# A two-block network on one core: where the first stage makes its low weight parts, and in which order its last projection reads its input

## The chip, the cores and the metric

The kernel runs on one core of a Trainium2 chip. Its time is the device time of one execution in microseconds (us); the number used is the median of the runs shown. The engines are named as the profile names them: PE multiplies matrices (PEld is its weight load), DVE is the vector engine, ACT the scalar engine, POOL is GpSimd, SP the queue that issues most loads. L75 is line 75 of the kernel.

## The reference, cut to what matters

A sequence of 256 positions with 1024 channels passes through two blocks. The change lies in the first half of the first block:

```python
h = rms_norm(x, norm1_g)
q, k, v, a, g = split(h @ w_in, 5)            # five parts of 512 columns each
attn = neighbourhood_attention(q, k, v, rpb)
conv = conformer_conv(a, g, ...)              # a*sigmoid(g), 31 taps per channel, LayerNorm, silu
mixed = concatenate([rms_norm(attn), rms_norm(conv)])
x = x + mixed @ w_out
h = rms_norm(x, norm2_g)
x = x + expert_choice_ffn(h, ...)             # 16 experts, 24 MB of weights each
```

After it come a second attention with a gating branch, and 256 gathers of rows from a table of 16,384 experts.

## The kernel before, in words

**Products in two parts.** The first stage multiplies in a reduced format that keeps only the high part of an fp32 number. To keep precision each operand is split in a high and a low part, and each product is three matmuls: high by high, high by low, low by high (`TERMS`). A weight block of 128 x 1024 (four of them make one 1024 x 512 weight, `kp` 0 to 3) is split by `split_w`: ACT copies it to `wh` (L68), and another engine subtracts, `wl = w - wh` (L75). With `pool_every=n` every n-th subtraction goes to POOL, the rest to DVE. `wh` and `wl` have three buffers each, so a split can run three blocks ahead of PE.

**The order of the first stage.** The weights come in the order g, a, q, k, v, then `w_out` in two halves of 512 columns, with the 12 loads of `w_ada` (the modulation of the second block, tile `pa`, L270) spread between them. `proj_T` (matmuls at L93) makes g, a, q and k transposed, `proj_N` (L111) makes v and the last projection. In q, k and v all low parts are POOL's (`pool_every=1`); in g and a they are DVE's.

**What runs beside it.** After a and g, DVE computes the convolution of three of the four channel groups, one tap at a time: `acc` gets a first tap (L363) and 30 more (L366) for each group. The fourth group goes over PE with diagonal matrices made by ACT (`cdg`, L375, L376). The scores of the four head pairs (L430) go to DVE (L434, L436), the exponentials to ACT (L441), then transposes and products on PE (L452, L461). Convolution and attention are normed (`conv_norm`, `attn_norm`) and written by `mix_in` into `mixT`: chunks 0 to 3 hold the attention, 4 to 7 the convolution. `mix_in` makes the product on DVE (L418), the high part on ACT (L81), the low part on DVE (L82).

**The last projection.** `wo[0]` and `wo[1]` are the two halves of `w_out`. A block `kp` uses chunks 2kp and 2kp+1 of `mixT`, so blocks 0 and 1 belong to the attention, 2 and 3 to the convolution. Then `turn_rows` transposes the new `X` (L576), `pl` are the router's logits (L592), and the experts begin (L658, L693).

**What sets the order.** The text is written in program order, but a scheduler that works on the dependencies places each engine's instructions; each engine then runs its own list strictly in order. SP issues loads strictly in order too. A weight load waits until its slot is free: there are five slots of 2 MB (`wload`), and four more for the experts (`W2`) that open when the first stage's memory is given back.

The lines that the change touches in the calls before:

```python
for _ in proj_T(P1, wload(A["w_in"][0]), hl, q_evac, pool_every=1):
run(proj_N(P1, wo[0], mixT, res_evac(0), pool_every=2, order=(2, 3, 0, 1)))
```

Of the kernel before, what the change touches and what calls it, by code (L numbers as in the profile page):

```python
# [9 lines left out]
AF = mybir.ActivationFunctionType  # L10
# [26 lines left out]
def body(tc, A, out, x1_in=None, dump=None, parts="1234"):  # L37
# [3 lines left out]
    act = nc.scalar.activation  # L41
# [10 lines left out]
    def ps(shape=(128, 512), name="ps"):  # L52
        return PS.tile(list(shape), F32, name=name, tag="ps")

    def pq(shape=(128, 512), name="pq"):
        return PS.tile(list(shape), F32, name=name, tag="pp")
# [7 lines left out]
    def split_w(pl, raw, wl=None, pool_every=0, bufs=3):  # L64

        wh = pl.tile([128, 1024], F32R, name="wh", tag="wh", bufs=bufs)
        ref, both, he, le = gate.pop(0) if gate else (None, False, None, None)
        i = act(wh, raw, AF.Copy) if he is None else he.tensor_copy(out=wh, in_=raw)  # L68
        if both:
            after(i, ref)  # L70
        if wl is None:
            wl = pl.tile([128, 1024], F32R, name="wl", tag="wl", bufs=bufs)
        turn[0] += 1
        eng = le or (nc.gpsimd if pool_every and turn[0] % pool_every == 0 else nc.vector)
        i = eng.tensor_tensor(out=wl, in0=raw, in1=wh.bitcast(F32), op=OP.subtract)  # L75
        if ref is not None:
            after(i, ref)
        return wh, wl
# [5 lines left out]
    def proj_T(pl, wt, hl, evac, wl=None, pool_every=0):  # L84

        pp = [pq((128, 2, 256), name="pp") for _ in range(2)]
        for kp in range(4):
            wp = split_w(pl, wt[:, kp * 1024:(kp + 1) * 1024], None if wl is None else wl[:, kp * 1024:(kp + 1) * 1024], pool_every)
            for c in range(4):
                for k2 in range(2):  # L90
                    kd = kp * 2 + k2
                    for n, (a, b) in enumerate(TERMS):
                        mm(pp[c // 2][:, c % 2], lhsT=wp[a][:, k2 * 512 + c * 128:k2 * 512 + (c + 1) * 128],  # L93
                           rhs=hl[:, b, kd], start=kd == 0 and n == 0 and c % 2 == 0, stop=kd == 7 and n == 2,
                           skip_group_check=True)
            if kp < 3:
                yield
        for c2 in range(2):
            evac(c2, pp[c2])
        yield  # L100

    def proj_N(pl, wt, hl, evac, wl=None, pool_every=0, order=(0, 1, 2, 3)):

        pp = [pq(name="pp") for _ in range(2)]
        for i, kp in enumerate(order):
            wp = split_w(pl, wt[:, kp * 1024:(kp + 1) * 1024], None if wl is None else wl[:, kp * 1024:(kp + 1) * 1024], pool_every)
            for k2, t in ((0, 0), (0, 1), (1, 0), (1, 1)) if i < 3 else ((0, 0), (1, 0), (0, 1), (1, 1)):
                kd = kp * 2 + k2
                for n, (a, b) in enumerate(TERMS):
                    x = hl[b] if isinstance(hl, list) else hl[:, b]  # L110
                    mm(pp[t], lhsT=x[:, kd, t * 128:(t + 1) * 128], rhs=wp[a][:, k2 * 512:(k2 + 1) * 512],  # L111
                       start=i + k2 + n == 0, stop=i == 3 and k2 == 1 and n == 2)
            if i < 3:
                yield
        for t in range(2):
            evac(t, pp[t])
        yield

    def run(g):
        for _ in g:  # L120
            pass

    def after(ins, ref):

        tc.add_manual_dep(ins.ins, ref.ins.name, mybir.DependencyInfo(mybir.DependencyClass.Sync, mybir.DependencyReason.DATA),
                          reason="loads in the order of their use")
# [103 lines left out]
    def wload(src, n=4096, cut=1):  # L230
        if extra and extra.pop(0):
            t = W2.tile([128, 4096], F32, name="w", tag="w%d" % (3 - ring[2] % 4))
            ring[2] += 1
        else:
            i = ring[0] % ring[1]
            t = W.tile([128, 4096], F32, name="w", tag=("w", "w", "w", "wa", "wb")[i], bufs=3 if i < 3 else 1)
            ring[0] += 1
        dst = t[:, :n]
        if len(src.shape) == 3:
            dst = dst.rearrange("p (a b) -> p a b", a=src.shape[1])  # L240
        k = src.shape[1] // cut
        for i in range(cut):
            nc.sync.dma_start(out=dst[:, i * k:(i + 1) * k], in_=src[:, i * k:(i + 1) * k])
        return t
# [80 lines left out]
    if "1" in parts:  # L325
        p1 = ExitStack()
        P1 = p1.enter_context(pool(name="P1", bufs=1))
# [5 lines left out]
        hl = HP.tile([128, 2, 8, 256], F32R, name="h0", tag="h")  # L333
# [8 lines left out]
        def sl(c2):  # L342
            return slice(c2 * 2, c2 * 2 + 2)
# [4 lines left out]
        kT = P1.tile([128, 4, 256], F32, name="kT")  # L348
        vv = P1.tile([128, 2, 512], F32, name="vv")
# [38 lines left out]
                r = slice(hh * 64, hh * 64 + 64)  # L388
                act(qz[r, sl(c2), hh], p[r], AF.Copy)

        for _ in proj_T(P1, wload(A["w_in"][0]), hl, q_evac, pool_every=1):
            pass
        next(ad)
        run(proj_T(P1, wload(A["w_in"][1]), hl, lambda c2, p: act(kT[:, sl(c2)], p, AF.Copy), pool_every=1))

        next(ad)

# [67 lines left out]
        vev = []  # L465
        wv_ = wload(A["w_in"][2])
# [1 line left out]
        for i in range(4):  # L468
            nc.sync.dma_start(out=bias[:, i * 2:i * 2 + 2], in_=A["bias"][:, i * 2:i * 2 + 2])
        hps = [head_pair(hc) for hc in range(4)]  # L470
        for i, _ in enumerate(proj_N(P1, wv_, hl, lambda t, p: vev.append(act(vv[:, t], p, AF.Copy)), pool_every=1)):
            if i in (0, 2):
                next(hps[0])
            for _ in range(6):
                next(cv, None)
        mixT = HP.tile([128, 2, 8, 256], F32R, name="mixT", tag="h")
# [39 lines left out]
        wo = []  # L516
# [42 lines left out]
        def res_evac(b):  # L559
            def f(t, p):  # L560
                h = slice(b * 512, (b + 1) * 512)
                tt_(out=X[:, t, h], in0=p, in1=X[:, t, h], op=OP.add)
                after(act(hj[:, b, t * 512:(t + 1) * 512], X[:, t, h], AF.Square, accum_out=xss[:, t, b:b + 1]), early)
            return f
# [6 lines left out]
        def turn_rows(kp):  # L571
            p = ps((128, 2, 256))
            for k2 in range(2):
                for t in range(2):
                    kd = kp * 2 + k2
                    nc.tensor.transpose(p[:, k2, t * 128:(t + 1) * 128], X[:, t, kd * 128:(kd + 1) * 128], ident)  # L576
            act(h2[:, kp * 2], p[:, 0], AF.Copy)
            nc.vector.tensor_copy(out=h2[:, kp * 2 + 1], in_=p[:, 1])

        run(proj_N(P1, wo[0], mixT, res_evac(0), pool_every=2, order=(2, 3, 0, 1)))  # L580
        for i, _ in enumerate(proj_N(P1, wo[1], mixT, res_evac(1), pool_every=2)):
            if i in (1, 2):
                turn_rows(i - 1)
        turn_rows(2)
        turn_rows(3)
        pl = [pq((128, NE), name="pl") for t in range(2)]
# [246 lines left out]
    hl = HP.tile([128, 2, 8, 256], F32R, name="h1", tag="h")  # L833
# [11 lines left out]
    for t in range(2):  # L845
        i = nc.vector.tensor_scalar(out=xn[:, t], in0=X[:, t], scalar1=r2[:, t:t + 1], scalar2=None, op0=OP.mult)
# [126 lines left out]
    for kp in range(4):  # L973
        p = ps((128, 2, 256))
# [54 lines left out]
    for g2 in range(4):  # L1029
        p = ps((128, 2, 2, 128))  # L1030
        for g in range(2):
            for n in range(2):
                i = mm(p[:, g, n], lhsT=zv[:, n, (g2 * 2 + g) * 128:(g2 * 2 + g + 1) * 128], rhs=sws[:, g2 * 2 + g], start=True, stop=True)
# [17 lines left out]
    wo = [wload(A["w_out_2"][b]) for b in range(2)]  # L1051
    hl = HP.tile([128, 2, 8, 256], F32R, name="h2", tag="h")
# [459 lines left out]
```

## Time and profile before

| what | value |
|---|---|
| time, median of 3 runs (lowest to highest) | 2171.81 us (2170.49 to 2178.94) |
| the profiled execution's own time | 2175.27 us |
| its span, first to last instruction | 2173.3 us |
| busy PE, DVE, ACT, POOL | 1652.7, 918.4, 493.6, 509.8 us |
| mean DMA traffic | 361 GB/s |

The profiled execution is 3.46 us above the median. Part 2 of the page cuts the span in 40 slices of 54 us, each digit being busy tenths:

```profile
PE   7698767767666665555657999996888888887777
DVE  5934210000000000000006866766967766776754
POOL 3602100000000000000003311224555545554552
DMA  8578999999999999999996433436999999999996
GB/s 356 201 299 288 421 427 410 423 426 418 417 427 427 427 426 428 427 426 429 427 426 254 163 117 110 182 126 259 408 420 421 421 420 421 421 421 421 421 421 265
```

The first four slices are the first stage (up to some 204 us). From slice 5 to 22 the experts' weights come in at about 427 GB/s, then the second block follows, and from slice 28 on the gathers load DMA again. In the second slice PE, DVE and POOL are busy for 6 tenths and more while DMA moves only 201 GB/s.

### The profile page before, as it was taken

What the parts mean: (1) busy time and instruction counts of PE and PEld (TensorE: products, weight loads), DVE (VectorE), ACT (ScalarE), POOL (GpSimd) and SP (SyncE); (2) the same over time, 40 slices, a digit from 0 to 9 for tenths busy, and PEclk for the clock granted to TensorE, in tenths of its full rate; (3) what the DMA queues carried; (4) which work ended last, traced back from release to release, by engine and by line L of the source; (5) the groups of instructions that cost most, each with busy time, mean ns of one, the idle gap of its engine ahead of it and who ended that gap; (6) DMA issues with size and microseconds to landing.
All of it is one profiled execution on the core that took longest, in us unless ns stands there. A gap on an engine that the chain in (4) does not pass through costs nothing. (4 is left out here: it accounts for less than half of the span.)

```text
span 2173.3 us, 21500 instructions
## 1 busy us (share of the span) xinstructions
PE 1652.7 (76%) x8132; PEld 853.4 (39%) x8132; DVE 918.4 (42%) x1939; ACT 493.6 (23%) x985; POOL 509.8 (23%) x353
## 2 busy tenths in 40 slices
PE   7698767767666665555657999996888888887777
PEld 6555213222211111111115878985444433443332
DVE  5934210000000000000006866766967766776754
ACT  4373110000000000000004456642332222222111
POOL 3602100000000000000003311224555545554552
PEclk9898977889987788887888999997999999999998
DMA  8578999999999999999996433436999999999996
GB/s 356 201 299 288 421 427 410 423 426 418 417 427 427 427 426 428 427 426 429 427 426 254 163 117 110 182 126 259 408 420 421 421 420 421 421 421 421 421 421 265
DMA packets 81974, 784.90 MB, mean 361 GB/s; under 512 B 12752, under 2 KB 13136, under 8 KB 18640
## 3 DMA queue, kind: packets, MB, share of 16 engines
q1 hardware_dynamic: 39920, 508.25, 56.8%
q0 software_dynamic: 36864, 268.45, 29.8%
q10 hardware_dynamic: 5088, 6.84, 1.0%
q8 instruction: 64, 1.05, 0.2%
q14 instruction: 38, 0.31, 0.0%
HBM read 780.35 MB, written 3.16 MB: 361 GB/s over the span
## 5 line engine op out<-in xcount | busy, mean ns | idle before, releaser
L1329 PE MATMUL acc<-uv,dgu 128*128 128x512 f32 x1024 | 493.9, 639 | 119.1 <-ACT dgu L1327 119.0
L1303 POOL DMA_INDIRECT uv<-in_peer_uv_dram,ei x256 | 331.6, 1295 | 304.2 <-DMA uv<-in_peer_uv_dram,ei 149.9
L1311 DVE CUSTOM_DVE_ANT_0 uv<-uv,xn 128x1024 f32<-128x1024 f32 x256 | 313.3, 1225 | 150.6 <-DMA uv<-in_peer_uv_dram,ei 142.8
L1329 PEld LDWEIGHTS acc<-uv,dgu 128*128 128x128 f32 x1024 | 203.6, 204 | 380.2 <-issue 234.7
L710 PE MATMUL pd<-w,hidT 128*32 128x512 f32 x1024 | 175.9, 805 | 97.0 <-DMA w<-in_w_down_dram 89.5
L693 PE MATMUL pu<-w,xsT 128*32 128x512 f32 x1024 | 157.8, 745 | 101.3 <-DMA w<-in_w_up_dram 101.2
L693 PE MATMUL pg<-w,xsT 128*32 128x512 f32 x1024 | 154.1, 729 | 97.0 <-DMA w<-in_w_gate_dram 97.0
L699 DVE TENSOR_TENSOR hid<-pu,hid 128x512 f32<-128x512 f32 x16 | 11.1, 691 | 503.8 <-PE pu L693 470.0
L859 POOL MEMSET q2z<- 64x2048 f32 x1 | 1.8, 1798 | 865.4 <-PE pd L710 865.4
L93 PE MATMUL pp<-h,wh 128*128 128x256 f32 x896 | 172.3, 294 | 2.0 <-DVE h L82 1.1
L75 POOL TENSOR_TENSOR wl<-w,wh 128x1024 fp32r<-128x1024 f32 x34 | 106.5, 3133 | 242.7 <-ACT wh L68 242.3
L93 PEld LDWEIGHTS pp<-h,wh 128*128 128x128 f32 x896 | 145.2, 198 | 7.0 <-issue 1.9
L93 PE MATMUL pp<-h,wl 128*128 128x256 f32 x448 | 130.2, 291 | 22.5 <-POOL wl L75 19.8
L714 DVE COPY part<-pd 128x512 f32<-128x512 f32 x16 | 11.1, 692 | 283.1 <-PE pd L710 283.1
L68 ACT ACTIVATE wh<-w 128x1024 fp32r<-128x1024 f32 x99 | 104.1, 1058 | 94.0 <-PE pp L93 65.0
L710 PEld LDWEIGHTS pd<-w,hidT 128*32 128x32 f32 x1024 | 39.2, 130 | 217.3 <-DMA w<-in_w_down_dram 141.6
L693 PEld LDWEIGHTS pu<-w,xsT 128*32 128x32 f32 x1024 | 32.0, 124 | 223.1 <-DMA w<-in_w_up_dram 162.4
L1320 ACT ACTIVATE a<-dots 128x4 f32<-128x4 f32 (+1 forms) x66 | 13.6, 205 | 445.9 <-DVE dots L1311 445.9
L693 PEld LDWEIGHTS pg<-w,xsT 128*32 128x32 f32 x1024 | 30.5, 121 | 206.7 <-DMA w<-in_w_gate_dram 144.1
L698 ACT ACTIVATE hid<-pg 128x512 f32<-128x512 f32 x16 | 9.6, 597 | 446.5 <-PE pg L693 446.5
L75 DVE TENSOR_TENSOR wl<-w,wh 128x1024 fp32r<-128x1024 f32 x66 | 83.8, 1278 | 39.1 <-ACT wh L68 38.9
L93 PEld LDWEIGHTS pp<-h,wl 128*128 128x128 f32 x448 | 88.8, 198 | 23.5 <-POOL wl L75 20.4
(353 smaller groups left out, 2119.7 us busy)
## 6 DMA issues: line engine op xcount, KB each, us to landing
w<-in_w_up_dram SPq DMA_DIRECT2D x64, 2048.0 KB, 21.0
w<-in_w_gate_dram SPq DMA_DIRECT2D x64, 2048.0 KB, 21.1
w<-in_w_down_dram SPq DMA_DIRECT2D x63, 2048.0 KB, 21.6
w<-in_w_in_dram SPq DMA_DIRECT2D x22, 2048.0 KB, 8.6
w<-in_w_ada_dram SPq DMA_DIRECT2D x12, 2048.0 KB, 8.5
w<-in_w_out_dram SPq DMA_DIRECT2D x4, 2048.0 KB, 8.0
rw<-in_peer_w_query_dram SPq DMA_DIRECT2D x12, 512.0 KB, 8.4
w<-in_w_branch_attn_dram SPq DMA_DIRECT2D x2, 2048.0 KB, 7.6
```

Source lines behind the costliest of these rows:

```text
L68: i = act(wh, raw, AF.Copy) if he is None else he.tensor_copy(out=wh, in_=raw)
L75: i = eng.tensor_tensor(out=wl, in0=raw, in1=wh.bitcast(F32), op=OP.subtract)
L93: mm(pp[c // 2][:, c % 2], lhsT=wp[a][:, k2 * 512 + c * 128:k2 * 512 + (c + 1) * 128], rhs=hl[:, b, kd], start=kd == 0 and n == 0 and c % ...
L693: mm(p[j * 32:(j + 1) * 32, :], lhsT=xsT[:, kd, e * 32:(e + 1) * 32], rhs=w[:, k2 * 2048 + j * 512:k2 * 2048 + (j + 1) * 512], start=kd == ...
L698: first = act(hid, pg, AF.Silu)
L699: tt_(out=hid, in0=pu, in1=hid, op=OP.mult)
L710: mm(pd[h][j * 32:(j + 1) * 32, :], lhsT=hidT[:, q, j * 32:(j + 1) * 32], rhs=w[:, j * 1024 + h * 512:j * 1024 + (h + 1) * 512], start=q = ...
L714: nc.vector.tensor_copy(out=part[:, 512:1024], in_=pd[1])
L1303: nc.gpsimd.indirect_dma_start(out=r, out_offset=None, in_=UV, in_offset=bass.IndirectOffsetOnAxis(ap=eis[u][:, k:k + 1], axis=0))
L1311: nc.vector.tensor_tensor_reduce(out=x, in0=x, in1=hx[:, u % 2], scale=1.0, scalar=0.0, op0=OP.mult, op1=OP.add, accum_out=dots[:, j:j + 1])
L1320: act(a[:, 0:n], dots[:, 0:n], AF.Gelu)
L1329: mm(acc[t][b], lhsT=dg, rhs=r[:, D + b * 512:D + (b + 1) * 512], start=h == 0 and k == 0, stop=h == 7 and k == 15)
```

## The change

The three calls for q, k and v lose `pool_every=1`, so that their twelve low parts are made on DVE. The last projection no longer runs half by half with the convolution first in `wo[0]`; its two generators are stepped by hand: attention blocks of `wo[0]`, attention blocks of `wo[1]`, convolution blocks of `wo[0]`, convolution blocks of `wo[1]`. The transposes `turn_rows` 0 and 1 stand behind the last two steps.

```diff
-        for _ in proj_T(P1, wload(A["w_in"][0]), hl, q_evac, pool_every=1):
+        for _ in proj_T(P1, wload(A["w_in"][0]), hl, q_evac):
             pass
         next(ad)
-        run(proj_T(P1, wload(A["w_in"][1]), hl, lambda c2, p: act(kT[:, sl(c2)], p, AF.Copy), pool_every=1))
+        run(proj_T(P1, wload(A["w_in"][1]), hl, lambda c2, p: act(kT[:, sl(c2)], p, AF.Copy)))
...
-        for i, _ in enumerate(proj_N(P1, wv_, hl, lambda t, p: vev.append(act(vv[:, t], p, AF.Copy)), pool_every=1)):
+        for i, _ in enumerate(proj_N(P1, wv_, hl, lambda t, p: vev.append(act(vv[:, t], p, AF.Copy)))):
...
-        run(proj_N(P1, wo[0], mixT, res_evac(0), pool_every=2, order=(2, 3, 0, 1)))
-        for i, _ in enumerate(proj_N(P1, wo[1], mixT, res_evac(1), pool_every=2)):
-            if i in (1, 2):
-                turn_rows(i - 1)
+
+        g0 = proj_N(P1, wo[0], mixT, res_evac(0), pool_every=2)
+        g1 = proj_N(P1, wo[1], mixT, res_evac(1), pool_every=2)
+        for g in (g0, g0, g1, g1, g0, g0):
+            next(g)
+        for i in range(2):
+            next(g1)
+            turn_rows(i)
         turn_rows(2)
         turn_rows(3)
```

**DVE, from the end of the a projection to the taps.** `wl` are the low parts, `u` the gated input of the convolution, `acc` its sum. Before:

```order
L75 TENSOR_TENSOR wl<-w,wh 128x1024 x5
L353 TENSOR_TENSOR u<-pp,sg 128x2x256 x2
L363 TENSOR_SCALAR acc<-u,vec 128x256 x2
L366 SCALAR_TENSOR_TENSOR acc<-u,vec,acc 128x256 x60
L363 TENSOR_SCALAR acc<-u,vec 128x256
L366 SCALAR_TENSOR_TENSOR acc<-u,vec,acc 128x256 x15
```

The same place on DVE now:

```order
L75 TENSOR_TENSOR wl<-w,wh 128x1024 x7
L353 TENSOR_TENSOR u<-pp,sg 128x2x256 x2
L363 TENSOR_SCALAR acc<-u,vec 128x256
L75 TENSOR_TENSOR wl<-w,wh 128x1024
L366 SCALAR_TENSOR_TENSOR acc<-u,vec,acc 128x256
L363 TENSOR_SCALAR acc<-u,vec 128x256
L366 SCALAR_TENSOR_TENSOR acc<-u,vec,acc 128x256 x9
L75 TENSOR_TENSOR wl<-w,wh 128x1024
L366 SCALAR_TENSOR_TENSOR acc<-u,vec,acc 128x256 x3
L75 TENSOR_TENSOR wl<-w,wh 128x1024
L366 SCALAR_TENSOR_TENSOR acc<-u,vec,acc 128x256 x5
```

The two low parts of q's first blocks stand ahead of `u`, and each of the other ten stands between 3 to 10 taps; in this way it goes on to the last block of v, whose low part stands behind the first head pair's score `s` (L434).

**DVE, at the fourth head pair.** `s` are its scores, `st` its sums, `modT` a part of the second block's modulation, `rva` the variance of the convolution. Before:

```order
L75 TENSOR_TENSOR wl<-w,wh 128x1024 x2
L485 TENSOR_TENSOR acc<-acc,ps 128x256 x4
L434 SCALAR_TENSOR_TENSOR s<-ps,bias 128x512 x2
L436 TENSOR_REDUCE st<-s 128x2 x2
L281 TENSOR_TENSOR modT<-ps,vec 128x16 x2
L164 TENSOR_SCALAR rva<-ps 128x2
```

Now, behind the same pair's scores:

```order
L442 RECIPROCAL st<-st 128x2
L75 TENSOR_TENSOR wl<-w,wh 128x1024
L281 TENSOR_TENSOR modT<-ps,vec 128x16 x2
L164 TENSOR_SCALAR rva<-ps 128x2
L817 TENSOR_TENSOR gm_4311<-modT,vec 128x8
```

Before, this low part (the third of `w_out`) stood ahead of the fourth head pair's scores; it is now `wo[1]`'s first block, and ACT's high part for it stands between the pair's second and third exponential too.

**PE, at the start of the last projection.** `pp` are its sums, `dg` with `ones` spreads a row's scale over the partitions (convolution first, then attention), `sqs` with `ones` are the attention's sums of squares. Before:

```order
L413 MATMUL ps<-dg,ones 128x128 x2
L403 MATMUL ps<-ones,sqs 128x1 x8
L111 MATMUL pp<-wh,mixT 128x512 x3
L111 MATMUL pp<-wl,mixT 128x512
L111 MATMUL pp<-wh,mixT 128x512
L111 MATMUL pp<-wl,mixT 128x512
L111 MATMUL pp<-wh,mixT 128x512 x2
L111 MATMUL pp<-wl,mixT 128x512
L111 MATMUL pp<-wh,mixT 128x512
L413 MATMUL ps<-dg,ones 128x128
```

And now:

```order
L403 MATMUL ps<-ones,sqs 128x1 x8
L413 MATMUL ps<-dg,ones 128x128 x2
L111 MATMUL pp<-wh,mixT 128x512 x5
L111 MATMUL pp<-wl,mixT 128x512
L111 MATMUL pp<-wh,mixT 128x512
```

The attention's two `dg` products stood behind ten matmuls of the convolution's half; now they stand ahead of the first matmul of the projection. On POOL the row of 13 low parts shrinks to 1. SP's list of loads is the same in both.

## Rows read from the trace of the kernel before

**Rows 1.** PE in order of time, 52 to 77 us: start, length, engine, line, count.

```profile
52.80 0.40 PE L93 MATMUL pp<-h,wh 128*128 128x256 f32 x2
...
53.16 0.40 PE L93 MATMUL pp<-h,wh 128*128 128x256 f32 x2
72.25 0.58 PE L93 MATMUL pp<-h,wl 128*128 128x256 f32 x1 [18.69 <-POOL wl L75]
...
76.84 1.92 PE L270 MATMUL pa<-w,cT 128*32 128x512 f32 x16
```

**Rows 2.** POOL in order of time, up to 48 us.

```profile
43.70 2.38 POOL L75 TENSOR_TENSOR wl<-w,wh 128x1024 fp32r<-128x1024 f32 x1 [0.48 <-ACT wh L68]
```

**Rows 3.** POOL's instructions by line, 48 to 49 us: count | busy, mean ns | idle before.

```profile
L75 POOL TENSOR_TENSOR wl<-w,wh 128x1024 fp32r<-128x1024 f32 x1 | 23.5, 23522 | 2.6 <-ACT wh L68 2.6
```

**Rows 4.** Busy time by stretch: PE, PEld, DVE, ACT, POOL; PE's clock, DMA share, GB/s.

```profile
60.00:65.00 5.00, 0.00 (x0) 0.00 (x0) 5.00 (x14) 0.00 (x0) 5.00 (x1) 0.50 0.00 0
72.00:76.00 4.00, 3.75 (x17) 3.75 (x18) 3.93 (x3) 1.18 (x2) 4.00 (x3) 0.50 0.70 225
155.00:158.00 3.00, 3.00 (x20) 0.77 (x16) 0.00 (x0) 1.02 (x1) 0.00 (x0) 0.50 1.01 431
210.00:215.00 5.00, 5.00 (x37) 2.42 (x37) 0.75 (x1) 0.69 (x1) 0.00 (x0) 1.00 0.11 46
...
200.00:1220.00 1020.00, 681.96 (x3918) 233.66 (x3918) 137.03 (x204) 80.63 (x131) 38.10 (x28) 0.83 0.96 405
```

**Rows 5.** DVE in order of time, 13 to 107 us.

```profile
13.38 1.23 DVE L75 TENSOR_TENSOR wl<-w,wh 128x1024 fp32r<-128x1024 f32 x1
14.52 0.48 DVE L204 TENSOR_SCALAR hf<-ps,vec 128x256 f32<-128x256 f32 x1
...
42.68 0.69 DVE L353 TENSOR_TENSOR u<-pp,sg 128x512 f32<-128x512 f32 x1 [0.74 <-PE pp L93]
...
46.16 23.84 DVE L366 SCALAR_TENSOR_TENSOR acc<-u,vec,acc 128x256 f32<-128x256 f32 x60
...
96.16 0.69 DVE L434 SCALAR_TENSOR_TENSOR s<-ps,bias 128x512 f32<-128x512 f32 x1 [1.71 <-PE ps L430]
...
102.46 4.13 DVE L366 SCALAR_TENSOR_TENSOR acc<-u,vec,acc 128x256 f32<-128x256 f32 x8
106.51 1.28 DVE L434 SCALAR_TENSOR_TENSOR s<-ps,bias 128x512 f32<-128x512 f32 x2
```

**Rows 6.** DVE's taps by line: first 46 to 60 us, then 72.5 to 94.4 us.

```profile
L366 DVE SCALAR_TENSOR_TENSOR acc<-u,vec,acc 128x256 f32<-128x256 f32 x35 | 13.9, 482 | 0.0
...
L366 DVE SCALAR_TENSOR_TENSOR acc<-u,vec,acc 128x256 f32<-128x256 f32 x15 | 21.6, 1438 | 0.5
```

**Rows 7.** ACT in order of time, 50 to 142 us.

```profile
50.41 1.06 ACT L68 ACTIVATE wh<-w 128x1024 fp32r<-128x1024 f32 x1 [1.81 <-PE pp L93]
...
141.38 0.57 ACT L276 ACTIVATE m<-pa 128x512 f32<-128x512 f32 x1
```

**Rows 8.** PE in order of time, 163 to 191 us.

```profile
163.13 0.94 PE L111 MATMUL pp<-wh,mixT 128*128 128x512 f32 x3
...
166.28 0.40 PE L413 MATMUL ps<-dg,ones 128*128 128x128 f32 x2
...
187.36 0.39 PE L111 MATMUL pp<-wl,mixT 128*128 128x512 f32 x1
...
189.51 0.85 PE L576 MATMUL ps<-cst,X 128*128 128x128 f32 x6
```

**Rows 9.** DVE in order of time, 166 to 171 us.

```profile
166.72 1.26 DVE L418 SCALAR_TENSOR_TENSOR mf<-oT,vec,ps 128x256 f32<-128x256 f32 x3 [0.19 <-PE ps L413]
...
170.90 0.47 DVE L418 SCALAR_TENSOR_TENSOR mf<-oT,vec,ps 128x256 f32<-128x256 f32 x1
```

**Rows 10.** SP's load issues in order of time, 170 to 183 us.

```profile
170.05 0.33 SPq L243 DMA_DIRECT2D w<-in_w_gate_dram  x1
182.05 0.33 SPq L243 DMA_DIRECT2D w<-in_w_up_dram  x1
```

## The prediction

> **What bounds the kernel now.** I began with the digits of the page. From slice 5 on the expert weights fill DMA, so the first stage counts by when it lets the experts start. The stretches confirm it: over 200 to 1220 us DMA is at 0.96 of its share, while between 210 and 215 us it falls to 0.11 with PE busy throughout, since all slots are loaded and PE has only just begun to use them [rows 4]. From there on DMA waits for PE's start, and what comes earlier there ends earlier.
>
> Then I looked in the first stage for the engine that idles though it has work: PE in order of time. Its three-matmul groups of the q projection follow each other every 0.36 us (52.80 to 53.16), then it stands still for 18.69 us and waits for a low part from POOL [rows 1]. POOL's own rows say why: the subtraction takes 2.38 us when it runs alone [rows 2], and one that began under DVE's taps took 23.5 us [rows 3]. DVE was inside a run of 60 taps [rows 5] and never idle. During the wait DMA moved nothing (60 to 65 us), and PE's granted clock was 0.50, its 1.2 GHz level, and stayed there to 76 us [rows 4].
>
> **The change part by part.**
>
> *The wait goes.* Minus 18.69 us [rows 1]. The clock drop behind it goes as well. From 72.25 to 76.84 us PE ran the 21 matmuls left of q, 4.59 us [rows 1]; at 0.36 us for three they are 2.52 us, so another 2.1 us. Together 20.8 us, if the low parts come in time from DVE.
>
> *Do they come in time?* A low part on DVE takes 1.23 us and the next instruction starts 1.14 us after it began [rows 5]. Taps follow each other every 23.84/60 = 0.397 us when two channel groups alternate, and every 4.13/8 = 0.516 us when one group's chain is left [rows 5]. DVE is free at 43.4 us, when the second `u` is done (42.68 + 0.69) [rows 5]. From there by the new order: first tap and q's third low part to 44.9; eleven taps and q's fourth part, 44.9 + 4.4 + 1.1 = 50.5 us. PE needs it at 53.3, where it stopped before. k's first: three taps later, but its high part is on ACT until 51.5 (50.41 + 1.06) [rows 7]; done at 52.8, needed at 57.9 (q ends at 53.3 + 2.5, then 16 matmuls of `pa`, 1.92 us [rows 1]). A block of q or k is 24 matmuls, 2.88 us on PE, and between two low parts DVE has 3 to 10 taps, 1.2 to 4 us. Continued like this, k's fourth is there at 63.8 and needed at 66.5; v's first at 66.9 and needed at 71.4; v's last, behind the first head pair's score, at 77.4 and needed at 81.5. The smallest slack is some 2.5 us. So I count no stall of PE here; DVE reaches the first score at 75.5 us, against 96.16 minus 20.8 = 75.4 [rows 5].
>
> *What is late next.* The taps that stand between the first two head pairs: 16 of them, 38 in all to the third. The second pair's scores come on DVE at about 86.3 us; moved by 20.8 us they stood at 106.51 - 20.8 = 85.7 [rows 5]. ACT's exponentials wait for them: plus 0.6 us. Bounds: 0, if PE's diagonal products hide it, and 6.9 us, worked out under the second rival.
>
> *The third split of `w_out`.* It moves from a place where ACT and DVE were waiting into the fourth head pair's exponentials. ACT makes a high part in 1.06 us [rows 7], and `m`, for which PE waits, now comes behind one: PE's transposes of `m` are followed in its order by the convolution's sums, so that chain slips by 1.06 us and some of what DVE adds (1.23 us ahead of `modT` and `rva`). I take 1.7 us; bounds 0 (the slack between ACT's pieces) and 1.06 + 1.23 = 2.3 us.
>
> *The last projection.* PE began it at 163.13 us with the convolution's half and did ten matmuls before the first of the attention's two spreads; the second began at 166.28 [rows 8]. The attention's product came on DVE from 166.72 on, the last piece at 170.90 [rows 9]. Now PE has nothing to do until the attention's high part is there. The spreads run at once, at about 165.6 to 166.1; the products begin at some 166.4 (0.4 us each, three in 1.26) [rows 9], ACT's copy is 0.4 us: the first matmul is at 167.2 us. The sums: 96 matmuls stood with 8 transposes and 4 spreads from 163.13 to 187.59 (187.36 and one step) [rows 8], 24.5 us; less 12 small ones, 96 are 22.3 us. Now 4 transposes come in between (0.6 us), from 167.2: 190.1 us. On top comes the clock: PE does only the one-column sums of squares and four spreads for some 5 us ahead of 167.2. After the convolution's like sums the clock stood at 0.50, the 1.2 GHz level, from 155 to 158 us [rows 4]. Some 3.6 us of half pace cost 1.8 us. Bounds for the clock: 0, if it holds, and 2.1 us, as after the long wait. So 191.9 against 187.59: plus 4.3 us. Behind the last matmul four more transposes stand in front of the router, by 0.85 us for six [rows 8] plus 0.6 us.
>
> *Loads.* SP's order is unchanged, but `wo[0]`'s slot now comes free with its last low part, some 9 us later than the 170.05 us at which a gate load took it, and `wo[1]`'s about 2.5 us later than 182.05 [rows 10]. Behind it queue the loads for expert 0. PE itself is 5 us later here, so I take nothing; the DMA gap of 210 to 215 us [rows 4] covers it. Without that cover it would cost up to one load, 4.9 us at 427 GB/s.
>
> Sum: -20.8 + 0.6 + 1.7 + 4.3 + 0.6 = -13.6 us, so 2175.27 - 13.6 = 2161.7 for the profiled execution. That one lies 3.46 us above the median; from 2171.81 the forecast is 2158.2, rounded to **2158 us**. With the bounds (clock, split, pair) its own range is 2152 to 2163.
>
> **The rivals.**
>
> *The whole 20 us.* The last projection and the split cost nothing, because the attention is ready earlier than its old place in the queues shows: 2171.8 - 20.2 = 2151.6 us. For it: PE works through the old start without a long wait, and DVE's queue is emptier without POOL's subtractions. Against it: the attention's spread depends on `rva`, which stands behind the convolution's products on DVE in both orders.
>
> *DVE paces the stage.* Each tap takes 482 ns itself [rows 6], and the pace of 0.397 us holds only as long as the next one starts before the last has ended. The Trainium skill, "VectorE: DVE Perf Modes", section "The DRAIN you can't avoid", says that the next instruction cannot issue until the pipe has emptied; by that rule the pace is the duration. This trace differs, 60 taps in 23.84 us, and I go by it. At 0.482 us instead: 54 instructions up to the first score, each 0.085 us more, are 4.6 us, and with the next 16 at 0.482 to 0.6 us the second pair is 6.9 us late instead of 0.6. That gives 2158.2 + 6.3 = 2164.5 us. For it: low parts now break the alternating run nine times. Against it: the same row.
>
> *Nothing arrives.* The experts' DMA sets the end and would have begun no earlier: 2172 us. For it: 0.96 for 1000 us. Against it: the empty DMA at 60 to 65 and at 210 to 215 us [rows 4].
>
> *Slower: the low parts are starved on DVE.* Place: PE's 10 blocks from q's third to v's last, each behind taps in DVE's strict order. In the stretch from 72.5 to 94.4 us a tap took 1438 ns [rows 6]. I put that down to POOL's subtractions beside it; if it is DVE's own pace with one chain or with low parts between, v's last comes at 43.4 + 54 x 1.438 + 10 x 1.14 = 132 us instead of 81.5, 51 us late, and the time is 2158 + 51 = 2209 us. The gain of 13.6 us is gone from a pace of (81.5 + 13.6 - 43.4 - 11.4)/54 = 0.75 us per tap on. Against it: DVE ran 60 taps at 0.397 while POOL was the one that waited.
>
> **How the numbers follow.** Forecast 0.70, whole gain 0.15, DVE pace 0.07, nothing 0.03, starved 0.05. A run of this kernel tells about 0.5% from no change, 10.9 us, so faster means below 2160.9. About three quarters of the forecast's own range lie there: 0.53, and with the whole gain 0.68 faster. The same: 0.17 + 0.07 + 0.03 = 0.27. Slower: 0.05. The range from 2149 to 2167 holds the forecast, the whole gain and the DVE pace, 0.92 less their tails.
>
> **What would show it.** The 18.69 us row is gone, and q, k and v run through at clock 1.00 with the last `wl` on DVE near 77 us; no PE wait on a low part. The first head pair's score near 75.5 us, the second's near 86. PE idle by 3 to 4 us ahead of the first L111 of the last projection, then a stretch at clock 0.50. The first expert matmul some 13 to 14 us earlier than before, and DMA with a gap right after it. I am wrong if PE waits for `wl` on DVE, if the clock holds and the projection starts at once, or if the first expert moves and the end doesn't.

## The result and the profile after

The changed kernel took 2158.97 us (median of five, 2150.77 to 2160.18) against 2173.63 us: ratio 0.9922 [0.9897, 0.9946]. Repeated beside the experiments it took 2151.42 against 2174.13, 0.9904 [0.9889, 0.9919]. Faster, as forecast. The forecast's own ratio, 2158.0/2171.81 = 0.9936, lies inside the first interval and just outside the second: the gain is nearer to 20 us than to 14.

Busy time and digits of the page after (40 slices of its span of 2148.1 us):

```profile
PE 1647.5 (77%) x8132; PEld 850.3 (40%) x8132; DVE 907.8 (42%) x1951; ACT 494.0 (23%) x985; POOL 461.2 (21%) x341
...
PE   7998758776766566666567999985987887888776
```

DVE took over twelve subtractions (1.23 us each, 14.7 in all), and its busy time still fell, from 918.4 to 907.8 us. All else on it shrank by 25.3 us, about 2 us for each subtraction that left POOL; the 90 taps alone (L366) went from 52.7 to 38.9 us. DVE had been paying for POOL's subtractions; the experiments show how.

PE in order of time (start, length, engine, line, count): the end of q, and the attention's sums with the start of the last projection.

```profile
55.41 0.28 PE L93 MATMUL pp<-h,wl 128*128 128x256 f32 x1
55.62 1.93 PE L270 MATMUL pa<-w,cT 128*32 128x512 f32 x16
...
140.19 1.84 PE L403 MATMUL ps<-ones,sqs 128*128 128x1 f32 x16
144.51 1.23 PE L413 MATMUL ps<-dg,ones 128*128 128x128 f32 x4 [2.48 <-DVE dg L408]
146.76 1.65 PE L111 MATMUL pp<-wh,mixT 128*128 128x512 f32 x3 [1.02 <-ACT mixT L81]
```

q goes straight on into `pa`, 21.2 us earlier than in [rows 1]; no wait of PE on a low part is left in q, k or v. DVE in order of time:

```profile
45.09 3.65 DVE L366 SCALAR_TENSOR_TENSOR acc<-u,vec,acc 128x256 f32<-128x256 f32 x9
48.65 1.22 DVE L75 TENSOR_TENSOR wl<-w,wh 128x1024 fp32r<-128x1024 f32 x1
49.78 1.27 DVE L366 SCALAR_TENSOR_TENSOR acc<-u,vec,acc 128x256 f32<-128x256 f32 x3
...
74.94 0.69 DVE L434 SCALAR_TENSOR_TENSOR s<-ps,bias 128x512 f32<-128x512 f32 x1
75.55 1.22 DVE L75 TENSOR_TENSOR wl<-w,wh 128x1024 fp32r<-128x1024 f32 x1
...
85.05 1.38 DVE L434 SCALAR_TENSOR_TENSOR s<-ps,bias 128x512 f32<-128x512 f32 x2
```

Low parts cost 1.2 us each, among taps that keep the pace of [rows 5] (9 in 3.65 us). Busy time by stretch, to be set beside [rows 4]: PE, PEld, DVE, ACT, POOL; granted clock, DMA share, GB/s.

```profile
60.00:65.00 5.00, 5.00 (x44) 5.00 (x43) 5.00 (x12) 2.12 (x2) 0.00 (x0) 1.00 1.06 415
...
145.00:150.00 5.00, 3.98 (x12) 3.01 (x11) 3.57 (x10) 1.62 (x4) 0.00 (x0) 0.50 1.04 334
192.00:197.00 5.00, 5.00 (x50) 1.46 (x48) 0.00 (x0) 0.69 (x1) 0.00 (x0) 1.00 0.25 79
```

At 60 us the still stretch is gone, and DMA moves 415 GB/s there. At 145 us the new thin stretch stands, with the clock at 0.50, its 1.2 GHz level. The gap after the experts' start (0.11 of DMA before) is still there, at 0.25. Between the router's logits and the first expert PE waits for `cs`, a product of two 16x256 tiles on DVE from which the selection `oh` is made; `xs` is the experts' input, split in two parts as the weights are. PE there, after:

```profile
172.91 2.75 PE L596 MATMUL pl<-wr,h 128*128 128x16 f32 x24
...
183.29 0.39 PE L652 MATMUL ps<-cst,cs 16*128 16x16 f32 x2 [5.38 <-DVE cs L648]
184.56 2.05 PE L662 MATMUL ps<-oh,xs 128*128 128x512 f32 x4 [0.88 <-DVE oh L654]
```

and before:

```profile
202.35 0.39 PE L648 MATMUL ps<-cst,cs 16*128 16x16 f32 x2 [7.51 <-DVE cs L644]
203.61 0.76 PE L658 MATMUL ps<-oh,xs 128*128 128x512 f32 x1 [0.87 <-DVE oh L650]
```

The first expert starts 19.05 us earlier. The profiled pair differs by more at its end (25.2 us of span); 4.7 of the missing 6.2 us lie in the expert stage, from the first expert's first matmul to the start of the last one's sum: 952.4 us before, 947.7 after. Among the experiments this stage took 947.3 to 953.7 us, 949.1 where q, k and v are as before (the third run below), so those 5 us are not shown to come from the change.

### The profile page after: what moved, and what is told of

It is laid out like the page before. It is cut to its first block, busy times and chain, and to the rows that moved or that the text cites. A ratio compares the mean times of both kernels' runs of the same rounds, so it can differ in the third digit from the quotient of the medians.

```text
span 2148.1 us, 21498 instructions
## 1 busy us (share of the span) xinstructions
PE 1647.5 (77%) x8132; PEld 850.3 (40%) x8132; DVE 907.8 (42%) x1951; ACT 494.0 (23%) x985; POOL 461.2 (21%) x341
## 5 line engine op out<-in xcount | busy, mean ns | idle before, releaser
L75 DVE TENSOR_TENSOR wl<-w,wh 128x1024 fp32r<-128x1024 f32 x78 | 97.2, 1252 | 50.3 <-ACT wh L68 50.1
L75 POOL TENSOR_TENSOR wl<-w,wh 128x1024 fp32r<-128x1024 f32 x22 | 55.8, 2537 | 276.8 <-ACT wh L68 276.4
L1331 ACT ACTIVATE dgu<-cst,a 128x128 f32<-128x128 f32 x256 | 82.7, 391 | 34.7 <-DVE a L1326 27.6
## 6 DMA issues: line engine op xcount, KB each, us to landing
w<-in_w_gate_dram SPq DMA_DIRECT2D x64, 2048.0 KB, 21.2
```

What stands on the lines that cost most here:

```text
L1331: act(dg, ident, AF.Copy, scale=a[:, j:j + 1])
```

## The experiments

Each expectation names its own theory and its rival. Where one speaks of a pair that excludes each other, it means POOL's reads and DVE's two-operand instructions: the time is lost whichever of the two is held up.

**The whole change again**, as it stands, beside the three that follow.

> The whole change once more, on the same chip as the three below, to have a pair of times from one place. Theory: first expert matmul (L662) near 184.6 us as in the first profile (before: 203.6), end-to-end 14 to 20 us faster than before, ratio 0.991 to 0.994. Rival (the profile of the changed kernel was a lucky one): first expert at 186 to 187 us, because one DVE instruction of the routing (the product cs, 0.41 us in that profile, 2.55 us before) falls behind POOL's subtraction again.

2151.42 us, 0.9904 [0.9889, 0.9919]; the first expert starts at 184.8 us, and PE's wait for `cs` is 5.38 us again. The result and its path repeat.

**The low parts alone**: the kernel before, with `pool_every=1` taken from q, k and v.

```diff
-        for _ in proj_T(P1, wload(A["w_in"][0]), hl, q_evac, pool_every=1):
+        for _ in proj_T(P1, wload(A["w_in"][0]), hl, q_evac):
...
```

> Only the first half of the change: low parts of q, k and v on DVE, the last projection as before. Theory (PE stood for POOL's low part; the new projection order costs 4 to 5 us at its start): no PE wait on a low part, q ends near 55.6 us, the last projection starts 21 us earlier than before (142 instead of 163.1), without the 3.5 us wait ahead of it and without a stretch at clock 0.50; first expert 2 to 4 us earlier than with the whole change, 20 to 23 us before the old one. Time 2150 to 2156 if before is 2172. Rival (the order change brings its own gain): slower than the whole change by over 2 us.

2151.03 us, 0.9897 [0.9883, 0.991], the whole gain. The last projection started without a wait, with the clock at 1.00 from 140 to 150 us (PE in order of time):

```profile
141.78 0.93 PE L111 MATMUL pp<-wh,mixT 128*128 128x512 f32 x3
```

Its router was done 4.4 us before that of the changed kernel (171.27 against 175.66); the first expert started only 2.2 us earlier, since `cs` took 2.54 us here, and the last expert's sum began alike (1132.8 and 1132.3 us). So the new order of the projection costs some 4.4 us in its place, and no difference of that size is left at the end.

**The projection alone**: the changed kernel with `pool_every=1` put back at q, k and v.

```diff
-        for _ in proj_T(P1, wload(A["w_in"][0]), hl, q_evac):
+        for _ in proj_T(P1, wload(A["w_in"][0]), hl, q_evac, pool_every=1):
...
```

> Only the second half: the last projection begins both halves with the attention, low parts of q, k and v on POOL as before. Theory: the 18.7 us wait of PE stays; the last projection starts 4 to 5 us later than before (168 instead of 163.1) behind a PE idle time of some 3.5 us and with clock 0.50 for 3 to 4 us; first expert +2 to +5 us, time +2 to +5 us (2174 to 2177 against 2172). Rival (the new order is free or gains): time within 1 us of before, or faster.

2176.04 us, 1.0011 [1.0001, 1.0022]: no gain. But the 18.69 us wait was not there either. DVE, POOL and PE in order of time:

```profile
44.45 43.25 DVE L366 SCALAR_TENSOR_TENSOR acc<-u,vec,acc 128x256 f32<-128x256 f32 x60
...
88.05 7.78 DVE L366 SCALAR_TENSOR_TENSOR acc<-u,vec,acc 128x256 f32<-128x256 f32 x15
...
46.96 2.60 POOL L75 TENSOR_TENSOR wl<-w,wh 128x1024 fp32r<-128x1024 f32 x1 [2.59 <-ACT wh L68]
49.83 2.67 POOL L75 TENSOR_TENSOR wl<-w,wh 128x1024 fp32r<-128x1024 f32 x1 [0.27 <-ACT wh L68]
...
109.35 1.11 PE L279 MATMUL ps<-cst,m 128*128 128x128 f32 x4 [21.51 <-ACT m L276]
```

With the same order on DVE and POOL as before, POOL got through in 2.6 us where it had taken 23.5 [rows 3], and DVE's taps were held up: the 60 took 43.25 us against 23.84 [rows 5], 19.4 more beside nine subtractions, 2.2 us for each. PE ran q, k and v without that wait and stood still later for 21.51 us, at `m` (ACT's copy of `pa`), behind ACT, which waited for DVE's first scores. It is about the same price at another place: the last projection starts at 170.08 us, 23.3 after the changed kernel's, where the wait in q had made 21.2.

**Convolution first in both halves**: the changed kernel with

```diff
-        g0 = proj_N(P1, wo[0], mixT, res_evac(0), pool_every=2)
-        g1 = proj_N(P1, wo[1], mixT, res_evac(1), pool_every=2)
+        g0 = proj_N(P1, wo[0], mixT, res_evac(0), pool_every=2, order=(2, 3, 0, 1))
+        g1 = proj_N(P1, wo[1], mixT, res_evac(1), pool_every=2, order=(2, 3, 0, 1))
```

> The whole change, but both halves of the last projection begin with the convolution's blocks (2, 3) and end with the attention's (0, 1). Theory (PE idles only because the attention's half comes last): PE has 48 matmuls, 11 us, before it needs the attention, so no wait at all; projection starts near 142 us, no clock drop; first expert at or a little before that of the kernel with the low parts alone, 3 to 5 us before the whole change; time 4 us below it. Rival (something else than the attention's lateness holds the start, such as a split of w_out that is late): the start stays at 146 us or the gain is under 1 us.

2147.46 us, 0.9887 [0.987, 0.9903]; the projection starts at 141.78 us without a wait, the first expert at 180.7. The median lies 4 us under the whole change on the same chip; the intervals of the two ratios overlap.

**The same, and POOL's second `xs` after `cs`**:

```diff
-                nc.gpsimd.tensor_tensor(out=xs[:, 1, t], in0=xn2, in1=xs[:, 0, t].bitcast(F32), op=OP.subtract)
+                if t == 0:
+                    nc.gpsimd.tensor_tensor(out=xs[:, 1, t], in0=xn2, in1=xs[:, 0, t].bitcast(F32), op=OP.subtract)
...
-            tt_(out=cs, in0=cs, in1=sel, op=OP.mult)
+            i = tt_(out=cs, in0=cs, in1=sel, op=OP.mult)
+            after(nc.gpsimd.tensor_tensor(out=xs[:, 1, 1], in0=xn2, in1=xs[:, 0, 1].bitcast(F32), op=OP.subtract), i)
```

> The kernel with the convolution first in both halves, and POOL's second subtraction in the routing (xs) held back until DVE's product cs is done, so that the two can't meet. Theory (cs waits 2.1 us behind POOL's subtraction when that one starts first): cs 0.41 us, PE's wait for it 5.4 instead of 7.5 us, first expert near 178.6 us instead of 180.7, time 1 to 3 us below conv first alone (2145 to 2147 at the same chip). Rival (cs is slow for another reason): cs stays at 2.5 us, no gain.

2146.12 us, 0.9868 [0.985, 0.9887]. What it is about, in the kernel before (DVE, then POOL):

```profile
199.75 2.55 DVE L644 TENSOR_TENSOR cs<-cs,sel 16x256 f32<-16x256 f32 x1
...
199.68 2.34 POOL L629 TENSOR_TENSOR xs<-xn,xs 128x1024 fp32r<-128x1024 f32 x1 [1.26 <-ACT xn L628]
```

and in the changed one:

```profile
182.82 0.41 DVE L648 TENSOR_TENSOR cs<-cs,sel 16x256 f32<-16x256 f32 x1
...
182.86 2.60 POOL L633 TENSOR_TENSOR xs<-xn,xs 128x1024 fp32r<-128x1024 f32 x1 [1.26 <-ACT xn L632]
```

Before, POOL began 0.07 us ahead of `cs`, and `cs` took 2.55 us; after, POOL began 0.04 us behind it, and `cs` took 0.41. Here the order holds it so: `cs` took 0.41 us, PE's wait was 5.38, and the first expert started at 175.9 us, 4.9 earlier than without the edit; 2.7 of these were there at the end of the router's sums (169.6 and 166.9). Both kernels once more on another chip, first the one without this edit:

> The kernel with the convolution first in both halves once more, on one chip with the next one. Theory (the routing's cs waits behind POOL's subtraction): PE's wait for cs 7.5 us, time 2146 to 2149. It is the base for the next.

> As the last, with POOL's second subtraction held back until cs is done. Theory A (a first expert that starts 2.2 us earlier ends 2.2 us earlier): time 2 us below conv first on the same chip. Theory B (DMA is without a gap by now, so the experts' weights set the end from here on): the first expert is 2 us earlier, the end of the experts and the time the same within 1 us.

They took 2148.54, 0.9904 [0.989, 0.9919], and 2145.4, 0.9887 [0.987, 0.9905]; `cs` took 2.54 us in the one and 0.41 in the other, PE's wait for it 7.51 and 5.38. The 2.1 us at the router are shown. The first expert moved by only 0.8 us this time (179.5 to 178.7), as the router's sums ended 1.4 later with the edit (168.4 and 169.7), ahead of the place that it touches. Whether the end gains is not settled, as the intervals overlap. This version has the lowest ratio of all, 0.9868, and then 0.9887, which the one without the edit had reached too; that second interval still overlaps the one of the change as it stands.

**Subtractions on POOL that nobody reads**, one behind each of the twelve low parts, in the changed kernel:

```diff
+        if 8 < turn[0] <= 20:
+            after(nc.gpsimd.tensor_tensor(out=scratch[0], in0=X[:, 0], in1=X[:, 1], op=OP.subtract), i)
...
```

The lines left out make the 128x1024 tile `scratch[0]`; the two experiments that follow have it too.

> The whole change, and behind each of the twelve DVE low parts of q, k and v one more subtraction on POOL, of the same size, on two old tiles, into a tile that nobody reads: POOL's old load is back, but no engine waits for it. Theory (subtractions on POOL and DVE's two-operand instructions exclude each other, so the price is paid by whoever starts second): DVE loses up to 2.2 us for each that POOL wins, up to 26 us in all, PE waits for late low parts, first expert at 195 to 207 instead of 184.7, time 10 to 22 us above the whole change. If POOL loses all of them, its subtractions take far over 2.4 us each (as the 23.5 us one before) and the time stays within 2 us. Rival (POOL is merely slow and only PE's wait for it cost time): each subtraction 2.4 us, taps at 0.40 us throughout, no change of time.

2175.71 us, 1.0017 [1.0004, 1.0031]. No engine waits for these subtractions, and the whole gain is gone: the time is 24.3 us above that of the next run, on the same chip, which lost nothing; 10 to 22 us were expected. POOL, DVE and PE in order of time:

```profile
53.45 2.52 POOL L78 TENSOR_TENSOR scr<-X 128x1024 f32<-128x1024 f32 x1 [4.99 <-DVE wl L76]
...
53.23 3.42 DVE L372 SCALAR_TENSOR_TENSOR acc<-u,vec,acc 128x256 f32<-128x256 f32 x3
...
97.13 0.79 PE L114 MATMUL pp<-wl,h 128*128 128x512 f32 x1 [3.92 <-DVE wl L76]
```

Three taps take 3.42 us instead of 1.27: 2.15 us for each subtraction. PE waits six times for low parts on DVE, 13.0 us in all, and the first expert starts at 209.0 us, 24.4 later than in the changed kernel; 2.1 of these are `cs`, which took 2.55 us here.

**The same with two memsets on POOL in place of a subtraction**:

```diff
+            after(nc.gpsimd.memset(scratch[0], 0.0), i)
+            after(nc.gpsimd.memset(scratch[0], 0.0), i)
```

> As the last, but two memsets of the same tile on POOL (about 1 us each) in place of each subtraction, which write and read nothing. Theory (it is the reading that excludes): taps stay at 0.40 us, memsets at about 1 us, time within 2 us of the whole change. Rival (any work of POOL on this memory excludes DVE): taps beside them 1 us longer, first expert later by up to 20 us.

2151.38 us, 0.9903 [0.9884, 0.9922]: nothing is lost. POOL and DVE in order of time:

```profile
51.28 0.95 POOL L78 MEMSET scr<- 128x1024 f32 x1 [3.92 <-DVE wl L76]
...
51.09 1.26 DVE L373 SCALAR_TENSOR_TENSOR acc<-u,vec,acc 128x256 f32<-128x256 f32 x3
```

Work on POOL that only writes leaves these two-operand taps alone (1.26 us for three, 1.27 without it).

**The same with a copy of one operand**:

```diff
+            after(nc.gpsimd.tensor_copy(out=scratch[0], in_=X[:, 0]), i)
```

> The whole change, and behind each of the twelve DVE low parts of q, k and v one copy of a tile of the same size on POOL, which nobody reads: one operand read instead of two, none in the memsets. Theory A (any reading by POOL excludes DVE's two-operand instructions for as long as it runs): a tap beside each copy is longer by the copy's time (some 1 to 2 us), 12 to 24 us on DVE in all, PE waits for low parts, time 5 to 20 us above the whole change. Theory B (only two operands collide): taps stay at 0.40 us and the time stays within 2 us of the whole change.

2161.29 us, 0.9963 [0.9947, 0.9979]: between the two.

```profile
51.02 1.17 POOL L78 COPY scr<-X 128x1024 f32<-128x1024 f32 x1 [4.98 <-DVE wl L76]
...
50.81 2.05 DVE L372 SCALAR_TENSOR_TENSOR acc<-u,vec,acc 128x256 f32<-128x256 f32 x3
```

Three taps take 0.78 us more beside a copy of 1.17 us, and the first expert starts at 196.4 us, 11.8 later, 2.1 of them by `cs` again. POOL's reading is what counts, by its length: the taps lose some 0.4 us less than the POOL instruction lasts, both here and beside the subtraction (2.15 of 2.52).

**The kernel before with the taps in one chain**, each group behind the last one:

```diff
+                        if i is not None:
+                            after(j, i)
+                        i = j
...
```

> The kernel before, with the taps of the three channel groups one group after another instead of two groups in turn, low parts of q, k and v still on POOL. One chain costs 0.516 us per tap instead of 0.397 and leaves a gap between taps. Theory A (the pair excludes each other whoever wins, so the lost time only moves): POOL's subtractions take 2.4 to 3 us, the 18.7 us wait for the low part of q is gone, but taps beside them take 1.2 us and more, and PE then waits for DVE (m behind the first scores) by about as much; time 0 to 10 us above before. Rival B (only the run of taps without a gap starved POOL): the wait is gone, nothing takes its place, time 10 us or more below before.

2175.36 us, 1.0013 [1.0002, 1.0024]. POOL took 2.4 to 2.6 us for each subtraction, the taps paid (DVE in order of time), and PE stood 22.04 us at `m`:

```profile
42.04 36.45 DVE L370 SCALAR_TENSOR_TENSOR acc<-u,vec,acc 128x256 f32<-128x256 f32 x30
...
78.97 15.59 DVE L370 SCALAR_TENSOR_TENSOR acc<-u,vec,acc 128x256 f32<-128x256 f32 x30
```

A second way of getting POOL through, and again no gain: 36.45 us for 30 taps with POOL's subtractions beside nearly all of them, 15.59 (0.52 each, a single chain's pace in [rows 5]) once they are done.

## Why the prediction was right, and where it was not

*The wait.* Forecast -20.8 us. The end of q moved by 76.84 - 55.62 = 21.2 us, 0.5 of which was there before the wait: -20.7. (Behind the wait the rows have 22 matmuls, not 21, which makes 0.1 us.) Clock and DMA recovered as forecast. The step was right in size, but it told only half of the cause. It read the trace as a slow POOL that makes PE wait, and took the 2.38 us of [rows 2] for a subtraction that runs alone. It did not run alone; DVE's second first tap stood beside it and paid, in the kernel before and after (DVE in order of time):

```profile
43.74 2.50 DVE L363 TENSOR_SCALAR acc<-u,vec 128x256 f32<-128x256 f32 x1
...
44.76 0.41 DVE L363 TENSOR_SCALAR acc<-u,vec 128x256 f32<-128x256 f32 x1
```

The projection alone and the single chain took that wait away without a gain, and the unread subtractions brought the loss back with nobody waiting for POOL. The loss is the exclusion between POOL's reads and DVE's taps; the 18.69 us are the place where it came out in that execution. The 23.5 us of [rows 3] stand in one trace only: every other subtraction of a low part on POOL, in all traces, took 2.3 to 3.4 us. For the change it comes to the same, as it takes the reads away; a change that only made PE wait less for POOL would have been forecast wrong by these rows.

*The low parts on DVE.* Forecast: first score at 75.5, v's last low part done at 77.4, no stall. Measured 74.94 and 75.55 + 1.22 = 76.77, no stall. The rivals of a slower DVE fell: from start to start the 9 taps take (3.65 - 0.48)/8 = 0.396 us each between low parts too, against a duration of 0.48 [rows 6]. The Trainium skill ("VectorE: DVE Perf Modes", "The DRAIN you can't avoid") says that the next one does not start until the pipe is empty, but the same paragraph adds that one which is not held starts earlier. The prediction took up the first sentence only; the trace agrees with the second. The 1438 ns of [rows 6] were POOL's doing, as I had put it down: in the projection alone, where POOL was done by then, the same 15 taps took 7.78 us, 0.52 each.

*Second head pair, +0.6; split of `w_out`, +1.7.* Both were 0. DVE took up the second pair's scores at 85.05 us, 21.5 earlier than before, and PE's work behind them began 21.2 earlier (106.85 to 85.63), the transposes of `m` too (142.04 to 120.82): no later than the 21.2 us by which q's end had moved. For the split I had priced a high part on ACT ahead of `m`, but not that DVE no longer has the low part ahead of the pair's scores: ACT's exponentials began 23.2 us earlier (140.88 to 117.66) and took up the 1.06 us.

*The last projection, +4.3.* Forecast: start 4.1 us later than its place (167.2 against 163.13), end 4.3. Measured, against a stage that moved by 21.2 us: start 4.8 later (163.13 to 146.76), end 4.4 (187.59 to 170.76, one step behind the last matmul each time), with the clock at 0.50 in 145 to 150 us. PE stood for 2.48 + 1.02 = 3.5 us ahead of it, as forecast. Right in mechanism and size; the low parts alone, without the wait and with the clock at 1.00, confirm it from the other side.

*The tail, +0.6.* The end of the router's sums moved from 192.49 to 175.66, as much as the projection's end: 0.

*Not in the sum.* `cs`, -2.1 us, by a shift of 0.1 us between two engines.

Together -20.7 - 0.5 + 4.4 - 2.1 = -18.9 us, against 19.05 measured at the first expert and -13.6 forecast. The forecast was 5.4 us short on the path: three terms of delay, 2.9 us, that slack took up, the 2.1 us of `cs`, and the 0.5 us ahead of the wait. That the first measured median came within 1 us of it is partly luck; the repetition is 6.6 us lower. The rival of the whole 20 us named the right total with a reason that is half wrong: the split cost nothing, but the projection did cost its 4.4 us. That nothing arrives is refuted. Whether all of it arrives is open: the low parts alone led the changed kernel by 2.2 us at the first expert and by nothing at the last, but the expert stage itself differs by more than 6 us among these runs.

## What to carry to other kernels

When a POOL instruction takes ten times its usual length beside DVE, or DVE's instructions take several times theirs beside POOL, don't ask which of them to unload but whether both read SBUF. If so, move the work to the engine that does it faster, even if that one is busy, and DVE's own busy time may fall. Before pricing a wait as gain, ask what the released engine does to the one that made it wait; here the wait moved twice without getting shorter. An added instruction that nobody reads is a cheap way to price such an exclusion.

## What the runs showed of the hardware

POOL's subtraction costs the two-operand taps of DVE 2.15 us, a copy 0.78, a memset nothing. The Trainium skill, "SBUF — State Buffer", section "Who interferes with whom", says that a VectorE instruction with two SBUF inputs contends with a GpSimd instruction that reads SBUF and not with one that only writes. The three unread runs agree. Of DVE's two-port modes it says that whichever issues first has the shared ports for its whole instruction; `cs`, which has two inputs, behaves so (2.55 us when POOL began first, 0.41 when it did). By the same section `tensor_scalar` can enter a mode that contends with writes as well; beside the memsets the one-input first tap took 0.82 us where it is 0.41 after:

```profile
43.30 0.82 DVE L370 TENSOR_SCALAR acc<-u,vec 128x256 f32<-128x256 f32 x1
```

The rule does not explain [rows 3]: there one subtraction was shut out over more than fifty taps, up to their end at 70 us, not over one. Nor does the order on the two engines decide it, as far as the profile places POOL's start: in the projection alone it is the same as before, POOL began 0.13 us after the start of a tap as it did before (46.96 against 46.83, and 48.67 against 48.54), and came through. What decides it stays open.
